# A pooling mixer's steps put in one written list, with its RMS norm and its spare accumulators rearranged

## The chip, the cores and the metric

The program runs on one core of a Trainium2 chip. The metric is the device time of one execution in microseconds (us); before the change its median over three executions is 1689.29 us. The engines meant below are TensorE (PE in the profile: matmuls and transposes, results into the PSUM accumulators), VectorE (DVE), ScalarE (ACT), GpSimd (POOL) and the DMA queues, of which SyncE's (SP) carries the weights. Each engine works through its own instructions in order and waits on semaphores for the others.

## The reference

One inference step of a two-layer decoder on 512 prompt tokens and 8 sample tokens (520 columns here), width 1024. Each layer is half a SwiGLU block, a token mixer, half a SwiGLU block. The mixer of layer 0 pools; that of layer 1 is sliding-window attention.

```python
x = x + 0.5 * _swiglu(_rmsnorm(x, norm_g[l, 0]), ...)
h = _rmsnorm(x, norm_g[l, 1])
# layer 0, _pool_mixer, for each of 4 groups of 256 channels with window w in (2, 4, 8, 16):
means.append((end[..., c0:c1] - start) / cnt)      # mean of the last w rows
diff = pooled - u                                  # (B, T, 4, 256)
mixed = einsum('btgc,gcd->btgd', diff, w_pool)     # a 256x256 product per group
out = mixed * scale
x = x + out
x = x + 0.5 * _swiglu(_rmsnorm(x, norm_g[l, 2]), ...)
```

## The kernel before

The residual lies transposed: eight tiles `x[m]` of 128 channels by 520 tokens. Matrix products keep fp32 accuracy by splitting each operand into a high and a low part (`xh`, `xl`; `wh`, `wl`): ACT copies the high part in the rounded type, DVE subtracts it from the source for the low part (`split`, lines 298 to 307), and PE does three products. Weights come in by SP, are split by ACT and DVE some pieces ahead of PE (`W.prefetch`, lines 226 and 227), and `W.stop` bounds how far ahead.

The stretch that the change touches starts in the last third of the first SwiGLU block (`ffn(0, ...)`, 344 to 372 us of the profile). For each `m` PE makes a down product, DVE multiplies it by the row of 1/rms (line 674, `u`) and adds it to `x[m]` (line 675), and `deferred` (line 711) splits `x[m]` for the mixer and adds its square to `acc` (lines 447 to 451). The last hidden tile of that block, `g`, is split into `hh` and `hl` at about 343 us and used by the first down products.

The mixer (lines 877 to 976) does for each of four groups: `zt`, thirty matmuls of 256 columns that multiply the tokens, in five parts of 128 (four of the prompt, a fifth for the last prompt rows and the samples), by the group's weights; `zt_evac`, five splits of these results scaled by 1/rms of each token (`zh` by ACT, `zl` by DVE); and `band`, which for each of two channel tiles does eleven matmuls with a band matrix (`th`, `tl`, `G`, `bt`) that does the pooling, two small ones for the samples, the addition to `x[m]` on DVE (lines 934 and 937), and the split of the new `x[m]` for the next block. `rstd_tok` sums `acc` over channels by five products with a column of ones (line 462) and takes 1/rms by a bit shift and three Newton steps on DVE. Two turned tiles (`hx`, lines 967 to 975) go out as the new pooling state.

What sets the order: a scheduler places every instruction on its engine by its own estimate of times, except those given to `later` (`keep_in_program_order`), which keep the written order among themselves. `seq` is `later` only while `ordered[0]` is true. The file defines `split` twice; the second definition, the one in force (lines 298 to 307 come from it), doesn't pass its two instructions through `seq`. In the mixer before, only the squares and a few steps are in written order. PSUM is eight banks, taken as four pairs (`duo`).

Of the kernel before, what the change touches and what calls it, by code (L numbers as in the profile page):

```python
# [18 lines left out]
P = 128  # L19
# [32 lines left out]
B_T = 520  # L52
B_W = 776

# [190 lines left out]
def yoco_step(ctx, tc, ins, outs):  # L245
# [33 lines left out]
    def seq(ins):  # L279

        return later(ins) if ordered[0] else ins
# [171 lines left out]
    pss_ = [None]  # L453
    nsb = [4]

    def rstd_tok(tiles=(0, P, 2 * P, 3 * P, 400)):
# [8 lines left out]
        seq(V.tensor_scalar(y.bitcast(I32), v.bitcast(I32), 1, None, op0=ALU.arith_shift_right))  # L465
        seq(V.tensor_scalar(y.bitcast(I32), y.bitcast(I32), -1.0, float(0x5F3759DF), op0=ALU.mult, op1=ALU.add))
        for it in range(3):
            seq(V.tensor_tensor(t_, y, y, op=ALU.mult))
            seq(V.scalar_tensor_tensor(t_, t_, -0.5, v, op0=ALU.mult, op1=ALU.mult))
            o = r_tok[:, :nt] if it == 2 else y  # L470
            seq(V.scalar_tensor_tensor(o, t_, 1.5, y, op0=ALU.add, op1=ALU.mult))

    def rstd_samples():
# [234 lines left out]
    def ff_pool():  # L708
        return tc.tile_pool(name="ff", bufs=2)

    def deferred(n, tmp, tag, tags, lst, w=TOK, hold=False):
# [166 lines left out]
    with tc.tile_pool(name="pm", bufs=2) as pm:  # L878
# [3 lines left out]
        tok0 = (0, 128, 256, 384, 400)  # L882
        r5 = pm.tile([P, 1], F32, name="r5", bufs=1)

        def zt(gi):

            pd = duo()
            banks = [pd[:, 0, :], pd[:, 1, :], ps()]
            wh, wl = prep["w", gi]
            views = []  # L890
            for tau in range(5):
                o = banks[tau // 2][:, (tau % 2) * 256 : (tau % 2) * 256 + 256]
                views.append(o)
                n = 0
                for kk in range(2):
                    xh, xl = mov1[2 * gi + kk]
                    s = slice(tok0[tau], tok0[tau] + P)
                    for a, b in ((xh, wh), (xh, wl), (xl, wh)):
                        T.matmul(o, a[:, s], b[:, kk, :], start=(n == 0), stop=(n == 5))  # L899
                        n += 1  # L900
            return views

        def zt_evac(views):
            zh = pm.tile([P, 5, 256], F32R, tag="zh", name="zh")
            zl = pm.tile([P, 5, 256], F32R, tag="zl", name="zl")
            for tau in range(5):
                split((zh[:, tau, :], zl[:, tau, :]), views[tau], r_tok[:, tau : tau + 1] if tau < 4 else r5)
            return zh, zl

        def band(gi, zz):  # L910

            zh, zl = zz
            Gt, (th, tl) = prep["G", gi], (prep["T", gi][:, 0, :], prep["T", gi][:, 1, :])
            G = lambda c: Gt[:, B_G + c : B_G + c + 256]
            for mi in range(2):
                m = 2 * gi + mi
                c = slice(mi * P, (mi + 1) * P)
                pd = duo()
                po, pso = pd[:, 0, :], pd[:, 1, :]
                pl = [(0, zh, th), (0, zl, th), (0, zh, tl), (1, zh, G(0)), (1, zl, G(0))]  # L920
                pr = [(1, zh, G(256)), (1, zl, G(256)), (2, zh, G(128)), (2, zl, G(128)), (3, zh, G(0)), (3, zl, G(0))]
                for half, lst in ((0, pl), (1, pr)):
                    for i, (tau, z, b) in enumerate(lst):
                        T.matmul(  # L924
                            po[:, half * 256 : half * 256 + 256],
                            z[:, tau, c],
                            b,
                            start=(i == 0),
                            stop=(i == len(lst) - 1),
                        )  # L930
                bs = Gt[:, B_S : B_S + NS]
                T.matmul(pso[:, :NS], zh[:, 4, c], bs, start=True, stop=False)
                T.matmul(pso[:, :NS], zl[:, 4, c], bs, start=False, stop=True)
                V.scalar_tensor_tensor(
                    x[m][:, SP:], pso[:, :NS], gcol(N_PS, m), x[m][:, SP:], op0=ALU.mult, op1=ALU.add
                )
                V.scalar_tensor_tensor(
                    x[m][:, :SP], po, gcol(N_PS, m), x[m][:, :SP], op0=ALU.mult, op1=ALU.add
                )
                z = pair(XX, [P, TOK])  # L940
                split(z, x[m], gcol(2, m))
                mov2.append(z)

        mov2 = []
        hx = pm.tile([P, KT, P], F32, name="hx", bufs=1)
        for k in range(KT):
            S.activation(hx[:, k, 0:120], x[k][:, 400:520], AF.Copy, scale=gcol(1, k))
# [19 lines left out]
        for a in range(2):  # L967
            pt = ps()
            for k in range(4):
                T.transpose(pt[:120, k * P : (k + 1) * P], hx[:, a * 4 + k, 0:120], ident)  # L970
            hrow = splp.tile([120, 512], F32, tag="S", name="hrow", bufs=4)
            S.activation(hrow, pt[:120, :], AF.Copy, scale=r_tok[:120, 4:5])
            cols = slice(a * 512, (a + 1) * 512)
            nc.gpsimd.dma_start(pool_prompt[0, 0, :, cols], hrow[97:112, :])
            nc.gpsimd.dma_start(pool_sample[0, :, 14, cols], hrow[112:120, :])

    movk = []
    with ff_pool() as tmp:
# [717 lines left out]
```

## Time and profile before

| | us |
|---|---|
| median of the runs (lowest, highest) | 1689.29 (1687.31, 1690.34) |
| the profiled execution | 1684.47 |
| span of its trace | 1682.70 |
| PE busy | 1652.9 (98%) |
| DVE busy | 1241.7 (74%) |
| ACT busy | 889.5 (53%) |
| mixer, from its first matmul to the next block's first | 33.49 |

The mixer's length is 405.67 less 372.18 in the timeline. A busy engine in the profile isn't one at its peak: matmuls overlap, so the time of one is read from start to start, and a wait from the bracket behind a row, which gives the engine's idle time before it and what ended it.

### The profile page before, as it was taken

The numbers are of one execution on the slowest core, as the hardware profiler recorded it, in microseconds if no ns is written. First come the engines' busy times: TensorE is split into PE (matmuls) and PEld (weight loads), VectorE is DVE, ScalarE is ACT, GpSimd is POOL, SyncE is SP. The second block draws the span as 40 slices with busy tenths as digits, with TensorE's granted clock in tenths as the row PEclk, the third lists the DMA queues.
The fourth block names the chain that finished last, engine by engine and source line by source line (L and its number), as shares of the span: only waits on it lengthen the run. The fifth ranks groups of instructions, "written<-read, shape, count | busy, mean of one in ns | idle before, by whom it ended". The sixth has DMA issues, their size and how long they took to land.

```text
span 1682.7 us, 34382 instructions
## 1 busy us (share of the span) xinstructions
PE 1652.9 (98%) x13740; PEld 1641.2 (98%) x13740; DVE 1241.7 (74%) x2371; ACT 889.5 (53%) x1766; POOL 151.9 (9%) x203
## 2 busy tenths in 40 slices
PE   9999999999999999999999999999989999999997
PEld 8999999999999999999999999999879999999997
DVE  6866866887975875878775875884886785785776
ACT  5743643666652552556552552653785663463455
POOL 0101101000101101100101101100100100110100
PEclk9999999999999999999999999999989999999999
DMA  8546846652645855634745845744212555675641
GB/s 215 137 124 142 188 128 136 172 166 76 147 134 128 178 146 128 166 114 119 167 132 125 190 131 129 164 144 106 66 26 76 131 124 141 138 169 145 143 126 51
DMA packets 314540, 225.97 MB, mean 134 GB/s; under 512 B 9726, under 2 KB 290022, under 8 KB 314340
## 3 DMA queue, kind: packets, MB, share of 16 engines
q1 hardware_dynamic: 287870, 178.12, 37.6%
q0 software_dynamic: 22752, 40.56, 14.9%
q10 hardware_dynamic: 3758, 5.09, 1.0%
q8 instruction: 108, 1.77, 0.4%
q14 instruction: 52, 0.43, 0.1%
HBM read 180.30 MB, written 5.04 MB: 110 GB/s over the span
## 4 chain that ended last, share of the span: by engine, by line
PE 94%; DVE 3%; ACT 2%; DMA 0%; issue 0%; ACTq 0%; DVEq 0%; SPq 0%; POOLq 0%
PE ps L524 45%; PE ps L498 42%; PE ps L1287 1%; ACT sm L1235 1%; PE ps L924 1%; PE ps L1257 1%; ACT xh L303 0%; PE ps L899 0%; PE ps L1203 0%; PE ps L1570 0%; PE ps L1577 0%; DVE wl L227 0%; PE ps L462 0%; PE ps L1381 0%; PE ps L783 0%
## 5 line engine op out<-in xcount | busy, mean ns | idle before, releaser
L226 ACT ACTIVATE wh<-raw 128x512 fp32r<-128x512 f32 (+1 forms) x730 | 442.9, 622 | 535.7 <-PE ps L498 319.1
L227 DVE TENSOR_TENSOR wl<-raw,wh 128x512 fp32r<-128x512 f32 (+1 forms) x730 | 484.1, 678 | 215.5 <-ACT wh L226 212.0
L524 PE MATMUL ps<-th,wh 128*128 128x260 f32 x1216 | 343.7, 283 | 0.0
L524 PE MATMUL ps<-tl,wh 128*128 128x260 f32 x1216 | 342.9, 282 | 0.0
L524 PE MATMUL ps<-th,wl 128*128 128x260 f32 x1216 | 341.4, 282 | 0.0
L498 PE MATMUL ps<-hh,wh 128*128 128x260 f32 x1340 | 271.4, 284 | 0.6 <-ACT vtok L1080 0.6
L498 PE MATMUL ps<-hl,wh 128*128 128x260 f32 x1340 | 271.4, 283 | 0.0
L498 PE MATMUL ps<-hh,wl 128*128 128x260 f32 x1340 | 269.1, 282 | 0.0
L524 PEld LDWEIGHTS ps<-tl,wh 128*128 128x128 f32 x1216 | 229.0, 188 | 0.0
L524 PEld LDWEIGHTS ps<-th,wh 128*128 128x128 f32 x1216 | 228.7, 188 | 0.0
L524 PEld LDWEIGHTS ps<-th,wl 128*128 128x128 f32 x1216 | 228.0, 188 | 0.0
L498 PEld LDWEIGHTS ps<-hl,wh 128*128 128x128 f32 x1340 | 207.7, 189 | 0.0
L498 PEld LDWEIGHTS ps<-hh,wh 128*128 128x128 f32 x1340 | 206.0, 189 | 1.2 <-ACT vtok L1080 0.9
L498 PEld LDWEIGHTS ps<-hh,wl 128*128 128x128 f32 x1340 | 206.6, 189 | 0.0
L524 PE MATMUL ps<-xh,wh 128*128 128x260 f32 x672 | 188.2, 283 | 0.0
L524 PE MATMUL ps<-xl,wh 128*128 128x260 f32 x672 | 188.0, 282 | 0.0
L524 PE MATMUL ps<-xh,wl 128*128 128x260 f32 x672 | 184.1, 281 | 0.0
L186 POOL DMA_DIRECT2D raw<-raw x76 | 65.5, 862 | 1297.5 <-DVE wl L227 484.8
L498 PE MATMUL ps<-xh,wh 128*128 128x260 f32 x736 | 149.1, 285 | 0.9 <-ACT wh L226 0.9
L498 PE MATMUL ps<-xl,wh 128*128 128x260 f32 x736 | 149.6, 284 | 0.2 <-DVE xl L802 0.2
L498 PE MATMUL ps<-xh,wl 128*128 128x260 f32 x736 | 147.9, 283 | 0.1
L674 DVE TENSOR_TENSOR u<-ps,R 128x520 f32<-128x520 f32 x93 | 64.9, 699 | 100.4 <-PE ps L498 100.4
(297 smaller groups left out, 2863.8 us busy)
## 6 DMA issues: line engine op xcount, KB each, us to landing
raw<-in_ffn_w_gate_dram SPq DMA_DIRECT2D x87, 512.0 KB, 3.9
raw<-in_ffn_w_up_dram SPq DMA_DIRECT2D x87, 512.0 KB, 5.4
raw<-in_ffn_w_down_dram SPq DMA_DIRECT2D x32, 1024.0 KB, 5.2
raw<-raw POOLq DMA_DIRECT2D x76, 256.0 KB, 3.3
S<-in_ffn_w_up_dram SPq DMA_DIRECT2D x76, 256.0 KB, 5.5
S<-raw POOLq DMA_DIRECT2D x76, 256.0 KB, 4.7
raw<-in_ffn_w_down_dram SPq DMA_DIRECT2D x16, 768.0 KB, 4.6
raw<-in_w_q_dram SPq DMA_DIRECT2D x8, 512.0 KB, 4.2
```

What stands on the lines that cost most here:

```text
L186: G.dma_start(blk(raw, 2, 1), blk(raw, 1, 1), accum_op=ALU.add)
L226: pin(nc.scalar.activation(dh, src, AF.Copy))
L227: pin(nc.vector.tensor_tensor(dl, src, dh.bitcast(F32), op=ALU.subtract))
L498: ins = T.matmul(banks[:, hf, :H], a[:, kk, :], hcols(b, hf), start=(first and i == 0), stop=(last and i == 2),)
L524: T.matmul(bank[:, :H], a[:, kk, :], b, start=(not more and kk == 0 and i == 0), stop=(kk == 3 and i == 2), skip_group_check=more,)
L674: pin(V.tensor_tensor(parts(u), bank[:, hfs[0] : hfs[-1] + 1, :H], parts(R[:, c]), op=ALU.mult))
L924: T.matmul(po[:, half * 256 : half * 256 + 256], z[:, tau, c], b, start=(i == 0), stop=(i == len(lst) - 1),)
L1235: S.activation(z, z, AF.Exp, scale=-1.0, bias=nm[:, i : i + 1], accum_out=self.den[:, i : i + 1])
L1257: T.transpose(both[:, bi, kt * 256 + e * P : kt * 256 + (e + 1) * P], self.sms[2 * bi + e][:, kt * P : (kt + 1) * P], ident,)
L1287: T.matmul(po[:, bi * 256 : (bi + 1) * 256], a, p_[:, kc_], start=(n == 0), stop=(n == 3 * len(kts) - 1),)
```

## The change

- A table `MPLAN` of 77 steps replaces the calls of the mixer. Each step is a letter and a number: Z and Y (a group's four parts and its fifth part), n (the norm), h (one copy into `hx`), e (one split of a result), B (a band), x (its addition to `x[m]`), s (the split of the new `x[m]`), q (its square), t (a turned tile), w (one piece of weights ahead), u (a load of the Silu table). While it runs, `seq` keeps the written order, so matmuls, additions, copies, squares and weight pieces are in it. The instructions of `split` (steps e and s) are not, for the reason above.
- The square of the last `x` tile is no longer added to `acc` by DVE. ACT writes it to a tile `held` (POOL clears its eight spare columns), and five more products with ones sum it.
- In this norm alone 1/rms comes from a square root on ACT, a reciprocal on DVE and one Newton step, in place of the shift and three steps. The Sqrt table is loaded by a step written behind the block's fourth down product; Silu's is loaded again by step u0.
- The four groups' fifth parts share one pair of banks, `fifth`, in place of a pair each.
- The five pieces of weights for the next block that were split without a fixed place come by steps w1 to w5.

```diff
+MPLAN = """
+h2 h0 Z0 h4 h5 Y0 n0 e0 h6 Z1 Y1 h3 e2 h1 Z2 e4 Y2 e9 e5 e1 e3 B0 h7 x0 e7 e6 s0 e8 B1 x1 e14
...
@@ rstd_tok
-        for t, lo in enumerate(tiles):
-            seq(T.matmul(pss[:, t : t + 1], acc[:, lo : lo + P], ones[:, 0:1], start=True, stop=True))
+        parts = [acc] if last is None else [acc, last]
+        for i, z in enumerate(parts):
+            for t, lo in enumerate(tiles):
+                o = pss[:, i * 8 + t : i * 8 + t + 1]
+                seq(T.matmul(o, z[:, lo : lo + P], ones[:, 0:1], start=True, stop=True))
...
+        if last is not None:
+            later(V.scalar_tensor_tensor(v, pss[:, 8 : 8 + nt], 1.0 / D, v, op0=ALU.mult, op1=ALU.add))
+            later(S.activation(y, v, AF.Sqrt))
+            later(V.reciprocal(y, y))
...
+        steps = 3 if last is None else 1
+        for it in range(steps):
@@ deferred
+            if hold and k == 3:
+                later(S.activation(warm, ones[:, 0:1], AF.Sqrt))
             if hold and k == KT - 1:
-                square(k, tmp, tag, later)
+                held.append(big.tile([P, TW], F32, tag="hh", name="held"))
+                nc.gpsimd.memset(held[0][:, TOK:], 0.0)
+                later(S.activation(held[0][:, :TOK], x[k], AF.Square))
@@ the mixer
+        def zt(gi, taus):
+            if gi not in zviews:
+                pd = duo()
+                zviews[gi] = [pd[:, tau // 2, tau % 2 * 256 : tau % 2 * 256 + 256] for tau in range(4)]
+            if 4 in taus:
+                if not fifth:
+                    fifth.append(duo())
+                zviews[gi].append(fifth[0][:, gi % 2, gi // 2 * 256 : gi // 2 * 256 + 256])
...
-        z0 = zt(0)
-        rstd_tok()
-        z1 = zt(1)
-        V.tensor_scalar(r5, r_tok[:, 4:5], sel[:, 32:33], sel[:, 33:34], op0=ALU.mult, op1=ALU.add)
-        e0 = zt_evac(z0)
-        z2 = zt(2)
-        e1 = zt_evac(z1)
-        band(0, e0)
-        z3 = zt(3)
-        e2 = zt_evac(z2)
-        W.stop = 10**9
-        W.prefetch()
-        W.pin = later
-        band(1, e1)
-        e3 = zt_evac(z3)
-        band(2, e2)
-        band(3, e3)
-        for m in range(KT):
-            square(m, pm, "sq", later)
+        def prefetch(i):
+            W.stop = W.ng - 1 + i
+            W.prefetch()
+        W.pin = later
+        ordered[0] = True
...
+            "q": lambda n: square(n, pm, "sq", later),
+            "t": hx_turn,
+            "w": prefetch,
+            "u": lambda n: later(S.activation(warm, ones[:, 0:1], AF.Silu)),
+        }
+        for step in MPLAN.split():
+            steps[step[0]](int(step[1:]))
+        ordered[0] = False
+        W.stop = 10**9
```

The order that the built programs have is shown below at three places. SP keeps its order throughout; PE, ACT and DVE keep theirs outside this stretch, the start of the block behind it and the attention stage.

**First place: ACT near the end of the first block.** `wh` is a piece of weights, `G` a band matrix, `pr` its raw tile, `hh` the high part of the last hidden tile. Before:

```order
L226 ACTIVATE wh<-raw_4201 128x384
L837 DMA pr<-in_bands_dram 128x512
L303 ACTIVATE hh<-g 128x520
L226 ACTIVATE wh<-raw_4201 128x384
L863 ACTIVATE G<-pr 128x512 x2
```

The same place now:

```order
L234 ACTIVATE wh<-raw_4201 128x384
L738 ACT_TABLE_LOAD
L738 ACTIVATE warm<-ones 128x1
L861 DMA pr<-in_bands_dram 128x512
L311 ACTIVATE hh<-g 128x520
L234 ACTIVATE wh<-raw_4201 128x384
L887 ACTIVATE G<-pr 128x512 x2
```

The Sqrt table's load stands three rows ahead of `hh`, though it is written behind the fourth down product.

**Second place: DVE in the mixer, from the first band's addition to the last low part of group 2.** `x_81` to `x_83` are the tiles m = 0 to 2; `zl` from `ps_5026` (before) and `ps_5019` (now) are group 2's, from `r_4918` and `r_4919` its fifth part. Before:

```order
L937 SCALAR_TENSOR_TENSOR x_82<-ps_5090,gT,x_82 128x512
L307 SCALAR_TENSOR_TENSOR xl<-x_81,gT,xh 128x520
L307 SCALAR_TENSOR_TENSOR zl<-ps_5026,r_tok,zh 128x256
L307 SCALAR_TENSOR_TENSOR zl<-ps_5027,r_4918,zh 128x256
L307 SCALAR_TENSOR_TENSOR xl<-x_82,gT,xh 128x520
L307 SCALAR_TENSOR_TENSOR zl<-ps_5026,r_tok,zh 128x256 x2
L934 SCALAR_TENSOR_TENSOR x_83<-ps_5180,gT,x_83 128x8
L937 SCALAR_TENSOR_TENSOR x_83<-ps_5180,gT,x_83 128x512
L307 SCALAR_TENSOR_TENSOR zl<-ps_5026,r_tok,zh 128x256
```

Now:

```order
L315 SCALAR_TENSOR_TENSOR xl<-x_82,gT,xh 128x520
L457 COPY acc<-sq 128x520
L315 SCALAR_TENSOR_TENSOR zl<-ps_5019,r_tok,zh 128x256
L235 TENSOR_TENSOR wl<-raw_4483,wh 128x512
L962 SCALAR_TENSOR_TENSOR x_83<-ps_5127,gT,x_83 128x8
L962 SCALAR_TENSOR_TENSOR x_83<-ps_5127,gT,x_83 128x512
L315 SCALAR_TENSOR_TENSOR zl<-ps_5019,r_tok,zh 128x256
L235 TENSOR_TENSOR wl<-raw_4483,wh 128x512 x2
L315 SCALAR_TENSOR_TENSOR xl<-x_83,gT,xh 128x520
L315 SCALAR_TENSOR_TENSOR zl<-ps_5019,r_tok,zh 128x256
```

Three pieces of weights and the first square's copy have come in between group 2's low parts.

**Third place: ACT in the attention stage, at about 1241 us.** `sm` is a softmax tile, multiplied by `den`; `oT` is the copy of a finished value product out of PSUM. Before:

```order
L303 ACTIVATE xh<-ps_16165 128x512
L1306 COPY oT<-ps_16196 64x256 x2
L1246 ACTIVATE sm<-sm,den 128x256 x2
L1363 ACTIVATE pr,smx<-ps_16206,smx 128x128
L1364 ACTIVATE smx<-sink_s,smx 128x1
```

Now:

```order
L311 ACTIVATE xh<-ps_16164 128x512
L1283 ACTIVATE sm<-sm,den 128x256 x2
L1343 COPY oT<-ps_16195 64x256 x2
L1400 ACTIVATE pr,smx<-ps_16205,smx 128x128
L1401 ACTIVATE smx<-sink_s,smx 128x1
```

The two multiplications have changed places with the two copies.

## Rows read from the trace of the kernel before

**Rows 1.** The page, part 1: busy us (share of span) and instructions.

```profile
PE 1652.9 (98%) x13740; PEld 1641.2 (98%) x13740; DVE 1241.7 (74%) x2371; ACT 889.5 (53%) x1766; POOL 151.9 (9%) x203
```

**Rows 2.** PE's waits, whole span: us in total, times, longest.

```profile
PE ps L462 <- DVE acc L451: 1.8, 1, 1.8
...
PE ps L1257 <- ACT oT L1306: 1.5, 1, 1.5
```

**Rows 3.** Timeline of PE in the mixer: start, us, instruction, [idle before <- releaser].

```profile
372.18 0.29 PE L899 MATMUL ps<-th,xh 128*128 128x256 f32 x1
...
375.62 0.28 PE L899 MATMUL ps<-th,xl 128*128 128x256 f32 x1
377.69 1.25 PE L462 MATMUL ps<-ones,acc 128*128 128x1 f32 x10 [1.79 <-DVE acc L451]
378.80 0.36 PE L899 MATMUL ps<-th,xh 128*128 128x256 f32 x1
...
383.38 0.39 PE L899 MATMUL ps<-th,xh 128*128 128x256 f32 x1 [0.81 <-DVE zl L307]
...
388.42 0.36 PE L924 MATMUL ps<-bt,zh 128*128 128x256 f32 x1
...
396.23 0.36 PE L924 MATMUL ps<-bt,zh 128*128 128x256 f32 x1 [1.07 <-DVE x L937]
...
404.08 0.65 PE L970 MATMUL ps<-ident,hx 128*120 128x128 f32 x4 [0.21 <-ACT hrow L972]
...
405.67 0.49 PE L498 MATMUL ps<-xh,wh 128*128 128x260 f32 x2
```

**Rows 4.** Timeline of DVE up to the norm's result.

```profile
372.20 1.30 DVE L227 TENSOR_TENSOR wl<-raw,wh 128x512 fp32r<-128x512 f32 x2
...
376.84 0.70 DVE L451 TENSOR_TENSOR acc<-acc,sq 128x520 f32<-128x520 f32 x1 [0.76 <-ACT sq L447]
...
381.29 0.17 DVE L471 SCALAR_TENSOR_TENSOR r_tok<-nt,ny 128x5 f32<-128x5 f32 x1
```

**Rows 5.** Timelines of ACT, DVE and PE at the last hidden tile.

```profile
343.31 0.64 ACT L303 ACTIVATE hh<-g 128x520 fp32r<-128x520 f32 x1
...
343.98 0.70 DVE L304 TENSOR_TENSOR hl<-g,hh 128x520 fp32r<-128x520 f32 x1
...
344.45 0.72 PE L498 MATMUL ps<-hh,wh 128*128 128x260 f32 x4
...
345.15 0.48 PE L498 MATMUL ps<-hl,wh 128*128 128x260 f32 x2
```

**Rows 6.** Timeline of ACT at a Sqrt table load in the last block.

```profile
1646.59 0.71 ACT L1500 ACTIVATE xg<-x,gT 128x520 f32<-128x520 f32 x1
1647.32 1.28 ACT L1506 ACT_TABLE_LOAD   x1
1648.62 0.20 ACT L1506 ACTIVATE warm<-ones 128x1 f32<-128x1 f32 x1
1648.72 0.25 ACT L1490 COPY ys<-ps 128x128 f32<-128x128 f32 x1
```

**Rows 7.** Timeline of DVE in the mixer: low parts, a band's addition, a new split.

```profile
384.66 1.90 DVE L307 SCALAR_TENSOR_TENSOR zl<-ps,r_tok,zh 128x256 fp32r<-128x256 f32 x4 [0.15 <-ACT zh L306]
388.60 0.23 DVE L934 SCALAR_TENSOR_TENSOR x<-ps,gT,x 128x8 f32<-128x8 f32 x1 [2.04 <-PE ps L933]
388.74 0.74 DVE L937 SCALAR_TENSOR_TENSOR x<-ps,gT,x 128x512 f32<-128x512 f32 x1
...
390.90 0.75 DVE L307 SCALAR_TENSOR_TENSOR xl<-x,gT,xh 128x520 fp32r<-128x520 f32 x1
```

**Rows 8.** Timeline of ACT in the attention stage.

```profile
1241.44 0.73 ACT L1306 COPY oT<-ps 64x256 f32<-64x256 f32 x2
1242.20 0.91 ACT L1246 ACTIVATE sm<-sm,den 128x256 f32<-128x256 f32 x2
```

**Rows 9.** Windows: us, busy of PE, PEld, DVE, ACT, POOL, granted clock, DMA.

```profile
1250.00:1260.00 10.00, 10.00 (x64) 9.85 (x64) 7.14 (x36) 7.40 (x29) 0.00 (x0) 0.66 0.38 88
```

More of the change, by code (lines that the diff above doesn't have):

```diff
@@ L454, in yoco_step, with rstd_tok @@
     nsb = [4]
-    def rstd_tok(tiles=(0, P, 2 * P, 3 * P, 400)):
+    def rstd_tok(tiles=(0, P, 2 * P, 3 * P, 400), last=None):
         pss_[0] = duo()
@@ L709, in ff_pool @@
         return tc.tile_pool(name="ff", bufs=2)
+    held = []
     def deferred(n, tmp, tag, tags, lst, w=TOK, hold=False):
@@ L898, in zt @@
                     for a, b in ((xh, wh), (xh, wl), (xl, wh)):
-                        T.matmul(o, a[:, s], b[:, kk, :], start=(n == 0), stop=(n == 5))
+                        seq(T.matmul(zviews[gi][tau], a[:, s], b[:, kk, :], start=(n == 0), stop=(n == 5)))
                         n += 1
[L901 to L908, printed above, removed]
@@ L910, in band, with zt_evac @@
-        def band(gi, zz):
-            zh, zl = zz
+        zs = {}
+        def zt_evac(gi, tau):
+            if gi not in zs:
+                zs[gi] = tuple(pm.tile([P, 5, 256], F32R, tag=n, name=n) for n in ("zh", "zl"))
+            r = r_tok[:, tau : tau + 1] if tau < 4 else r5
+            split(tuple(z[:, tau, :] for z in zs[gi]), zviews[gi][tau], r)
+        bands_ = {}
+        def band(m):
+            gi, mi = m // 2, m % 2
+            zh, zl = zs[gi]
             Gt, (th, tl) = prep["G", gi], (prep["T", gi][:, 0, :], prep["T", gi][:, 1, :])
@@ L914, in band @@
             G = lambda c: Gt[:, B_G + c : B_G + c + 256]
[L915 to L942, printed above, removed]
@@ new lines, in band @@
+            c = slice(mi * P, (mi + 1) * P)
+            pd = duo()
+            bands_[m] = po, pso = pd[:, 0, :], pd[:, 1, :]
+            pl = [(0, zh, th), (0, zl, th), (0, zh, tl), (1, zh, G(0)), (1, zl, G(0))]
+            pr = [(1, zh, G(256)), (1, zl, G(256)), (2, zh, G(128)), (2, zl, G(128)), (3, zh, G(0)), (3, zl, G(0))]
+            for half, lst in ((0, pl), (1, pr)):
+                for i, (tau, z, b) in enumerate(lst):
+                    o = po[:, half * 256 : half * 256 + 256]
+                    seq(T.matmul(o, z[:, tau, c], b, start=(i == 0), stop=(i == len(lst) - 1)))
@@ new lines, in band, with band_evac, band_split @@
+            bs = Gt[:, B_S : B_S + NS]
+            seq(T.matmul(pso[:, :NS], zh[:, 4, c], bs, start=True, stop=False))
+            seq(T.matmul(pso[:, :NS], zl[:, 4, c], bs, start=False, stop=True))
+        def band_evac(m):
+            po, pso = bands_.pop(m)
+            for c, p_ in ((slice(SP, TOK), pso[:, :NS]), (slice(0, SP), po)):
+                seq(V.scalar_tensor_tensor(x[m][:, c], p_, gcol(N_PS, m), x[m][:, c], op0=ALU.mult, op1=ALU.add))
+        def band_split(m):
+            z = pair(XX, [P, TOK])
+            split(z, x[m], gcol(2, m))
+            mov2.append(z)
@@ L959, in yoco_step, with hx_copy, norm @@
-        W.prefetch()
-        W.pin = later
-        band(1, e1)
-        e3 = zt_evac(z3)
-        band(2, e2)
-        band(3, e3)
-        for m in range(KT):
-            square(m, pm, "sq", later)
-        for a in range(2):
+        def hx_copy(k):
+            seq(S.activation(hx[:, k, 0:120], x[k][:, 400:520], AF.Copy, scale=gcol(1, k)))
+        def norm():
+            rstd_tok(last=held[0])
+            seq(V.tensor_scalar(r5, r_tok[:, 4:5], sel[:, 32:33], sel[:, 33:34], op0=ALU.mult, op1=ALU.add))
@@ L975, in yoco_step @@
             nc.gpsimd.dma_start(pool_sample[0, :, 14, cols], hrow[112:120, :])
+        def prefetch(i):
[3 more added lines that the diff above has]
+        ordered[0] = True
+        steps = {
+            "Z": lambda n: zt(n, range(4)),
+            "Y": lambda n: zt(n, (4,)),
+            "n": lambda n: norm(),
+            "h": hx_copy,
+            "e": lambda n: zt_evac(n // 5, n % 5),
+            "B": band,
+            "x": band_evac,
+            "s": band_split,
+            "q": lambda n: square(n, pm, "sq", later),
[7 more added lines that the diff above has]
+        W.stop = 10**9
     movk = []
```

27 lines of the change are left out of this document (12 added, 15 removed).

## The prediction

> **What bounds the kernel now.** I read the page first, then PE's waits, then the timelines of the stretch that is changed. PE is busy 98% of the span [rows 1], so a change pays where PE waits. In the mixer it does so four times [rows 3]: 1.79 us for the sum of squares, 0.81 for a low part, 1.07 for an addition to `x`, 0.21 for a turned tile. From its first matmul at 372.18 to the next block's first at 405.67 the mixer lasts 33.49 us. Nothing else in the change shortens PE's work, so the gain is bounded by the waits in this stretch. Read from start to start they are a little longer: the hole before the norm is 377.69 − 375.62 = 2.07, less 0.12 for the matmul itself, so 1.95; 0.16 more than the row's idle time. With as much added to the next two the four come to 3.88 + 0.48 = 4.4 us. That is 0.26% of the time, little over the 0.2% that a measurement of this kernel can tell from no change.
>
> **The change part by part.**
>
> *The norm's wait, and what comes in its place: −1.95 and +1.1.* Before, PE waited for DVE's last addition to `acc`, which itself waited for ACT's square [rows 2, 4]. Now the last square is not added but multiplied. It ends about where the addition began, 376.84, and the five pieces of weights that the scheduler had put between the last tiles, 0.65 us each [rows 4], move into the mixer, so DVE is earlier still unless it is held up elsewhere. PE gets to the norm at 375.74 at the earliest, spends some 1.1 us on the products with `acc`, and needs the square at 376.85. So this wait goes whole. The price is five more products: the ten records of the present five take 378.80 − 377.69 = 1.11 us [rows 3], so +1.1. The shorter chain behind it (about eight steps for thirteen; now 381.29 + 0.17 − 378.80 = 2.7 us after the products [rows 3, 4]) saves about 1 us, but PE has sixty matmuls of groups 1 and 2 to do meanwhile, some 7 us, so in itself it is worth nothing.
>
> *The other mixer waits: −2.45, and new ones: +2.6.* Sixty matmuls and not thirty now stand between the norm and the first band, so the waits of 0.81 and 1.07 go from where they are, and the turned tiles stand where their copies are long done. But DVE and ACT must do as much as before and more: four of the five pieces of weights, the first squares and a table load now come inside the bands. I priced the DVE rows of the second place by hand. From the norm to group 2's last low part DVE does fifteen low parts of 0.475 (1.90 for four), three band additions of about 0.9, three new splits of 0.75 [rows 7], three weight pieces of 0.65 [rows 4] and a copy of about 0.4: 7.1 + 2.7 + 2.25 + 1.95 + 0.4 = 14.4. The norm's chain of 1.6 and the first high part, 0.5, come ahead of it, and it idles about 1.7 before the first band's result, which stands behind the first ten low parts (it waited 2.04 there before [rows 7]): 18.2 in all. PE needs for its part 60 + 30 matmuls at 0.118 (thirty from 372.18 to 375.74) and four bands at 1.5 (388.42 is the second band's start, and thirteen matmuls follow): 10.6 + 6.0 = 16.6. So PE waits about 1.6 before the fifth band. Between the fifth and the seventh band PE has two bands and four turns, 3.7; DVE has five more low parts, an addition, a weight piece, a split and an addition to `acc`, 2.4 + 0.9 + 0.65 + 0.75 + 0.7 = 5.4, less what it has begun: another 1.2 to 1.7. These durations overlap by some 0.08 us from row to row (the first addition takes 0.23, but the next starts 0.14 after it [rows 7]); over the 28 and 10 rows that is 2.2 and 0.8 us back. The bounds are therefore 0.9 with all the overlap and 3.3 with none, and 4.4, the waits of before, if the two engines are held up as often as then. I take 2.6, nearer to the upper side, because the rows of before show these two engines in turn waiting for each other (0.15 and more a time), which the sum of durations leaves out.
>
> *The Sqrt table's load: +1.1.* It is placed three rows ahead of `hh`. At the nearest switch to this table [rows 6] ACT's next work starts 2.13 us after the start of the copy before it, 0.62 of which is the copy's own share: 1.5 us. `hh` would start at 343.31 + 1.5 = 344.8 and end at 345.46; PE wants it at 344.45 [rows 5]. The wait is 1.1 with the semaphore's delay. `hl` follows at once, 345.5 to 346.2, and PE, which takes 0.70 between its use of `hh` and of `hl`, finds it just done. DVE and ACT run behind PE for the rest of this block, so nothing hides that, and the whole remainder moves by 1.1. The bounds are 0, if ACT's waits for the band matrices come out earlier than before, and 1.5. The Trainium skill, on the page "ScalarE: Activation LUTs", section "What ACT_TABLE_LOAD costs", gives about 1.28 us for the load and about 1.38 more for a drain, 2.66 a switch. The load's 1.28 is the trace's; of a drain the rows show 0.1 us. By the skill's figure this term would be 2.5, and the sum 1.4 higher.
>
> *Attention: +0.8.* PE waits there 1.51 us for the copies `oT` [rows 2]. Now the two multiplications stand ahead of them, 0.91 us [rows 8], of which ACT overlaps about 0.1. Their inputs come no later than before. Bounds 0 and 0.9.
>
> *At no cost.* The fifth parts' common pair: a part is rewritten only a whole group of matmuls later, behind its evacuation. SP keeps its order; the weights of the fourth Strassen chunk are loaded some 25 us later because their buffer comes free when the last weight piece is split, but three plain tiles of PE's work, over 30 us, lie ahead of their use. POOL gets a clearing that nobody waits for.
>
> *Sum:* −4.4 + 1.1 + 2.6 + 1.1 + 0.8 = +1.2 us. On the profiled execution, 1684.47, that is 1685.7; the median of the runs lies 4.8 above it, so 1689.29 + 1.2 = **1690.5**.
>
> **The rivals.**
>
> *The list does what it is written for.* The four waits go, PE is never short of operands in the bands, and neither the table load nor the swap in the attention is felt because ACT reaches both early: −4.4 + 1.1 = −3.3, and 0.4 more if the turned tiles, which no longer alternate with band matmuls, run closer: 1685.6. For it: ACT is busy only 53% [rows 1]. Against it: the splits are not in the list, and DVE and ACT have more between the bands than before.
>
> *The norm's wait stays.* DVE is the late engine at the block's end and is now itself moved by the table load; if it loses the 1.5 us whole, the last tile is no earlier against PE and 1 to 1.9 us of the wait remain: 1692.0. Within 0.2%.
>
> *Slower: the clock.* In the attention stage PE's clock was granted at 0.66 over 1250 to 1260 [rows 9], that is, about 6.8 us at 1.2 GHz and not 2.4, behind a run of waits of which the 1.51 us one is the last large. Such a stretch costs half its length, 3.4 us. The waits in the mixer, up to 1.79, drew none. If the longer wait of 2.3 brings one stretch more of that length, the time is 1690.5 + 3.4 = 1693.9. It decides once some 4.4 us more are at the low level, since half of them is what the forecast leaves to 1692.7.
>
> *Slower: each switch holds ACT twice.* If ACT stands as long again as the load's own row, 1.28 us [rows 6], for each of the two loads, `hh` comes 2.4 us late, and Silu's load, which stands between the low parts of the last group, adds as much before the seventh band: 1690.5 + 2.6 = 1693.1. Rows 6 speak against it: what follows the load starts 1.30 after it. The rule of the Trainium skill cited above ("ScalarE: Activation LUTs") says that it is so.
>
> **How the numbers follow.** Forecast, within 0.2% (1685.9 to 1692.7): 0.61. The norm's wait stays, also within: 0.11. The list as written: 0.13, faster. The clock: 0.11, slower. The double hold: 0.04, slower. So faster 0.13, no change 0.72, slower 0.15. The unknown terms reach from 0.9 to 4.4 (bands), 0 to 1.5 (load), 0 to 0.9 (attention): 1686.9 with all low, 1692.8 with all high. To hold 8 in 10 the range takes in part of the cases on both sides, 1686.0 to 1694.0; it leaves out most of the first rival and the upper half of the clock's.
>
> **What would show it.** In the trace of the changed kernel: PE has no wait before the products with ones, which are twenty records over 2.2 us. PE waits about 1.1 us for `hh` at 344.5, behind a table load on ACT. PE waits one to one and a half us before the fifth and the seventh band, for `zl`. In the attention the wait for `oT` is 2.2 to 2.3 us. The forecast falls if the wait for `hh` is absent, if the bands run without a wait, or if the windows of the attention stage show more time at the low clock.

## The result

| | before | after |
|---|---|---|
| median of 22 runs, us (lowest, highest) | 1687.63 (1681.60, 1692.19) | 1692.22 (1685.88, 1694.99) |
| ratio, 95% interval | | 1.0024 (1.0012 to 1.0035) |
| the profiled execution, us | 1684.47 | 1690.16 |
| span of its trace, us | 1682.70 | 1688.3 |

The changed kernel is slower by 0.24%, 4.0 us (2.0 to 5.9). The forecast was 1.2 us slower, counted as no change within 0.2%; the measured time lies inside the range that was given and has the sign of the forecast, but it is three times as far and beyond the 0.2%, a case that the prediction gave 0.15. A second set of twelve runs of the changed kernel gave 1.0026 (1.0013 to 1.0040).

The executions of one kernel scatter over 9 to 11 us, and most of that goes with the granted clock: fitted over all runs of this study, an execution with 0.001 less in its mean granted clock is 1.2 to 1.3 us longer. The means agree, 0.9906 over 93 runs of the kernel before and 0.9905 over the 22 of the changed one, so the clock is not the difference. It does make two profiles hard to subtract: the traces hold stretches at the low level (granted clock 0.5), which lie elsewhere in each execution. Below, starts of the same matmul are compared only between such stretches.

### The profile page after: what moved, and what is told of

The parts are those of the page before. It is cut to its first block, busy times and chain, and to the rows that moved or that the text cites. A ratio compares the mean times of both kernels' runs of the same rounds, so it can differ in the third digit from the quotient of the medians.

```text
span 1688.3 us, 34402 instructions
## 1 busy us (share of the span) xinstructions
PE 1658.6 (98%) x13750; PEld 1646.5 (98%) x13750; DVE 1240.2 (73%) x2364; ACT 892.2 (53%) x1771; POOL 152.0 (9%) x204
## 4 chain that ended last, share of the span: by engine, by line
PE 92%; ACT 3%; DVE 3%; DMA 2%; issue 1%; ACTq 0%; POOL 0%; DVEq 0%; POOLq 0%; SPq 0%
PE ps L542 45%; PE ps L516 42%; PE ps L927 1%; ACT sm L1272 1%; PE ps L1324 1%; DMA S<-raw 1%; PE ps L954 1%; ACT wh L234 0%; ACT xh L311 0%; PE ps L1607 0%; PE ps L474 0%; PE ps L1240 0%; PE ps L1294 0%; DVE xl L312 0%; DMA S<-in_ffn_w_up_dram 0%
```

## The profile after

Part 1 of the page of the changed kernel, which answers to [rows 1]; PE is busy 5.7 us longer, in an execution that is 5.7 us longer:

```profile
PE 1658.6 (98%) x13750; PEld 1646.5 (98%) x13750; DVE 1240.2 (73%) x2364; ACT 892.2 (53%) x1771; POOL 152.0 (9%) x204
```

PE's waits in the changed kernel (us in total, times, longest), for [rows 2]. The wait for `acc` is gone; waits for `zl`, `wh` and `hh` are new. At the place of the attention stage where [rows 2] has 1.5 us for `oT` (line 1257, now 1294), PE waits 1.1 us for a low part of DVE's:

```profile
PE ps L954 <- DVE zl L315: 2.6, 2, 1.7
...
PE ps L542 <- ACT wh L234: 1.3, 2, 1.1
...
PE ps L1294 <- DVE xl L312: 1.1, 1, 1.1
...
PE ps L516 <- ACT hh L311: 0.7, 1, 0.7
```

Timelines at the last hidden tile, for [rows 5]. The load (1.28 us, as in [rows 6]) and the small activation behind it hold `hh` until 348.77, and PE stands idle 0.70:

```profile
347.36 1.28 ACT L738 ACT_TABLE_LOAD   x1
348.66 0.20 ACT L738 ACTIVATE warm<-ones 128x1 f32<-128x1 f32 x1
348.77 0.62 ACT L311 ACTIVATE hh<-g 128x520 fp32r<-128x520 f32 x1
...
349.44 0.74 PE L516 MATMUL ps<-hh,wh 128*128 128x260 f32 x4 [0.70 <-ACT hh L311]
```

From start to start the changed kernel falls 0.9 us further behind here: this row stands 4.99 behind its counterpart in [rows 5], the matmuls just before it 4.1.

Timeline of PE in the mixer, for [rows 3]:

```profile
377.42 0.28 PE L927 MATMUL ps<-th,xh 128*128 128x256 f32 x1
...
380.97 1.17 PE L474 MATMUL ps<-ones,acc 128*128 128x1 f32 x10
382.00 1.25 PE L474 MATMUL ps<-ones,held 128*128 128x1 f32 x10
383.11 0.37 PE L927 MATMUL ps<-th,xh 128*128 128x256 f32 x1
...
401.23 0.39 PE L954 MATMUL ps<-bt,zh 128*128 128x256 f32 x1 [0.90 <-DVE zl L315]
...
406.55 0.39 PE L954 MATMUL ps<-bt,zh 128*128 128x256 f32 x1 [1.74 <-DVE zl L315]
...
410.05 0.49 PE L516 MATMUL ps<-xh,wh 128*128 128x260 f32 x2
```

No bracket stands before the products; they take 383.11 − 380.97 = 2.14 us in place of 1.11. The four waits of before are replaced by two, before the fifth and the seventh band. The mixer lasts 410.05 − 377.42 = 32.63 us against 33.49: 0.86 shorter.

Forty microseconds later comes what the forecast did not have. Timelines of SP, POOL, ACT and PE, first before, then after:

```profile
372.93 0.37 SPq L318 DMA_DIRECT2D raw<-in_ffn_w_gate_dram  x1
...
376.95 16.54 SPq L989 DMA_DIRECT2D sink_s<-in_attn_sinks_dram  x8
416.84 0.39 SPq L318 DMA_DIRECT2D raw<-in_ffn_w_gate_dram  x1
...
435.22 1.83 POOL L185 DMA_DIRECT2D S<-raw  x2
```

```profile
404.34 0.37 SPq L326 DMA_DIRECT2D raw<-in_ffn_w_gate_dram  x1
...
408.64 15.56 SPq L1026 DMA_DIRECT2D sink_s<-in_attn_sinks_dram  x8
424.31 0.39 SPq L326 DMA_DIRECT2D raw<-in_ffn_w_gate_dram  x1
...
440.70 0.63 ACT L234 ACTIVATE wh<-S 128x512 fp32r<-128x512 f32 x1 [3.44 <-DMA S<-raw]
...
441.87 1.73 POOL L193 DMA_DIRECT2D S<-raw  x2 [2.14 <-PE ps L516]
...
450.87 0.39 PE L542 MATMUL ps<-xh,wh 128*128 128x260 f32 x1 [1.11 <-ACT wh L234]
```

SP's order is the same, but its first row here had to wait until the last weight piece was split, 404 and not 373. Twelve small copies (state, caches, sinks) stand behind that row, some 19 us of SP, and the next weights behind the copies. Before, the copies ran while SP had nothing else to do. Now they push the weights from 416.84 to 424.31. Part of that is the distance between the two profiles, so the places are better counted from the block's first matmul (405.67 and 410.05): the weights come 14.3 us behind it and not 11.2, POOL's sums `S` 31.8 and not 29.6. ACT stands 3.44 us for a piece of `S`, is then behind with its splits, and PE waits: 1.3 us from start to start.

## Experiments

Each ratio is to the kernel before on the same chip; 11 or 12 runs each, except the one noted. A time under the changed kernel "by the ratios" is taken from 1.0026, the second set on that chip, for the runs of the two edits, and from 1.0024 for the list with the old norm.

**The changed kernel again.**

> The changed kernel once more, beside the next three. Theory (places): its trace has the same three new waits of PE, 0.7 us for hh near 349 us, 2 and 1 us before two bands, 1.1 us for wh near 449.5 us, within 0.2 each, and the time is 1 to 4 us above the kernel before. Rival (clock): the places hardly matter, and the time goes with the mean granted clock: 0.990 to 0.992 here against 0.994 for the kernel before, 1.7 us for each 0.001.

1692.26 us, 1.0026 (1.0013 to 1.0040). The waits came back: 1.0 for `hh`, 2.7 for `zl`, 1.2 for `wh`. The mean granted clock of its runs is 0.9906. The clock rival falls, the places stand.

**The Sqrt load tied to the fourth square.**

```diff
-            if hold and k == 3:
-                later(S.activation(warm, ones[:, 0:1], AF.Sqrt))
...
+                sq = square(k, tmp, tag)
+            if hold and k == 3:
+                later(S.activation(warm, sq[:, 0:1], AF.Sqrt))
```

> The Sqrt table's load is tied to the fourth square, so that it can't be placed ahead of hh. Theory: PE's wait for hh near 349 us is gone (0.7 us idle, 0.85 in the starts), the load sits between squares where DVE is the later engine, and the time is 0.8 us under that of the changed kernel. Rival (late engine): the load now delays the squares, DVE's last addition comes 1 us later, PE waits for the products with ones again, 0.5 to 1.3 us, and nothing is gained.

1689.46 us, 1.0020 (1.0007 to 1.0033), 1.0 us under the changed kernel by the ratios. PE starts on `hh` without a wait, and none came before the products:

```profile
348.00 0.73 PE L517 MATMUL ps<-hh,wh 128*128 128x260 f32 x4
```

As the theory had it, for the trace; as a time 1.0 is less than the intervals can tell. The wait for `wh` near 449 us is absent in this profile too, though nothing was done to it. What explains it, as far as one trace can show, is a stretch at 1.2 GHz at the end of the mixer. Windows (us, busy of PE, PEld, DVE, ACT, POOL, granted clock, DMA) and PE's timeline there:

```profile
405.40:408.80 3.40, 3.40 (x19) 3.40 (x18) 3.40 (x8) 1.31 (x3) 1.08 (x2) 0.50 1.19 356
```

```profile
405.06 0.39 PE L955 MATMUL ps<-bt,zh 128*128 128x256 f32 x1 [1.77 <-DVE zl L315]
...
405.78 0.41 PE L955 MATMUL ps<-G,zl 128*128 128x256 f32 x1
406.00 0.41 PE L955 MATMUL ps<-G,zh 128*128 128x256 f32 x1
```

Two matmuls of 256 columns start 0.22 us apart here, against 0.12 at the high level, so the stretch cost PE some 1.5 us while SP, DVE and ACT went on. The late weights were then no longer late: one wait hid another. A wait that is absent from one profile is not proved cured.

**The copies ahead of the mixer.** The 12 DMAs of SP are written before the list, where SP waits for its buffer anyway.

```diff
+        later(nc.sync.dma_start(pool_sample[0, :, 0:14, :], state_pool[0, :, 1:15, :]))
...
         W.pin = later
         ordered[0] = True
...
-        later(nc.sync.dma_start(pool_sample[0, :, 0:14, :], state_pool[0, :, 1:15, :]))
```

> SP's copies of the state, the caches and the sinks (12 DMAs, some 15 us of SP) are written ahead of the mixer, where SP waits for a buffer, and not behind it. Theory (SP): the weights that followed the copies at 424 us come at about 409, the sum S on POOL by 427 and not 441, and PE's wait for wh at 449.5 us (1.1 us) goes: 1.1 us under the changed kernel. Rival (backlog): ACT and DVE are behind because four pieces were moved into the mixer; the sum comes early but PE waits 0.8 us or more for wh or hh in the same place.

1689.52 us, 1.0012 (1.0000 to 1.0024): 2.4 us under the changed kernel. The buffer comes free as late as there (402.85, in a profile that runs 1.5 us ahead of the changed kernel's here), but the weights behind it come at 417.88 and not 424.31, the sums at 436.80 and not 441.87; less the 1.5, that is 4.9 and 3.6 us earlier. PE has no wait between 444 and 452 us:

```profile
402.85 0.37 SPq L326 DMA_DIRECT2D raw<-in_ffn_w_gate_dram  x1
...
417.88 0.37 SPq L326 DMA_DIRECT2D raw<-in_ffn_w_gate_dram  x1
...
436.80 1.80 POOL L193 DMA_DIRECT2D S<-raw  x2
```

I had expected 409 for the weights and 427 for the sum; 436.80 was early enough. The wait for `hh` is still there, 1.13 us in this trace. The queue's copies were the cause, not a backlog of ACT.

**Both edits.**

> Both edits, the tied table load and the early copies. Theory (places): 2 us under the changed kernel, within 1.5 us of the kernel before on either side, and PE's starts behind 460 us stand where those of the kernel before stand, but for what the clock at the kernel's start makes. Rival (clock): the time stays with the changed kernel, 2 to 4 us above the kernel before, and its mean granted clock is 0.990 to 0.992.

1687.29 us, 1.0009 (0.9996 to 1.0023), 2.9 us under the changed kernel: the two edits add up within the intervals (1.0 and 2.4 alone). Neither wait is in its trace. Two thirds of the loss were these two waits, if the medians may be split so finely.

**The kernel before again, with a second profile.**

> The kernel before once more, with a profile of its own. Theory (places): outside the stretches at the low granted clock its PE stands within 0.3 us of the first profile of before all along, and the four waits of the mixer (1.8, 0.8, 1.1, 0.2) and that for oT in the attention return. Rival (one odd profile): the first profile was a lucky one, and this one is 1 to 3 us longer in stretches that the change does not touch, which would take as much from the difference between the two profiles.

1688.37 us, 0.9996 (0.9980 to 1.0011). Outside the low stretches and ahead of the attention stage its matmuls stand within 0.25 us of the first profile all along. So two profiles of one program can be laid on one another, and what is left over against the changed kernel needs a reason. In the attention they differ by 1 to 2 us. Its waits of PE:

```profile
PE ps L462 <- DVE acc L451: 2.3, 1, 2.3
...
PE ps L1257 <- ACT oT L1306: 0.6, 1, 0.6
```

The wait for `oT`, 1.5 in [rows 2], is 0.6 here in the same program. And behind the wait for `acc` there is a low stretch that the first profile did not have (window as above; it began at 381.9 and lasted 6.8 us):

```profile
381.00:389.00 8.00, 7.61 (x39) 7.64 (x40) 3.72 (x16) 3.44 (x12) 0.86 (x1) 0.57 0.77 279
```

**The list with the old norm.** The last square goes to `acc`, five products, shift and Newton steps; no table loads, no `held`.

```diff
-            rstd_tok(last=held[0])
+            rstd_tok()
...
-                held.append(big.tile([P, TW], F32, tag="hh", name="held"))
...
+                square(k, tmp, tag, later)
```

> The changed kernel with the norm of before: the last square is added to acc, five products, shift and three Newton steps, no table loads; the list stays. Theory (places): PE's wait for hh (0.85) and the five extra products (1.1) go, a wait for the last addition to acc comes back, 0.5 to 2 us, the longer chain costs nothing, the wait for wh near 449 us stays: 0 to 1.5 us under the changed kernel. Rival (norm pays): the wait comes back whole and the thirteen steps of DVE push the bands: 0.5 to 1.5 us above the changed kernel.

1690.30 us, 1.0012 (0.9997 to 1.0027), 2.0 us under the changed kernel. The wait before the products is back at 0.60 and a new one of 1.48 stands before the first band, whose splits now come behind the longer chain:

```profile
376.31 1.25 PE L474 MATMUL ps<-ones,acc 128*128 128x1 f32 x10 [0.60 <-DVE acc L459]
...
386.17 0.39 PE L950 MATMUL ps<-bt,zh 128*128 128x256 f32 x1 [1.48 <-DVE zl L315]
```

The wait for `wh` near 449 us, which the theory let stay, is 0.26 here. The mixer is as long as before. So the gain in the mixer is the new norm's, which the theory had wrong (the longer chain does cost), and yet the kernel without that norm is, if anything, faster. Part of that is the load. The rest showed when I laid this trace on the second one of before: they agree within 0.05 us from 43 us up to the mixer, and again from 454 us up to the attention, while the changed kernel's PE drifts away all along, in code that is the same. What does the new norm have that reaches so far?

**A wider buffer, and nothing else.** `held` is declared with 528 columns under the tag `hh`, whose other tiles have 520. One buffer size serves a tag, so all eight take 2112 bytes a partition, not 2080, and everything allocated behind them moves by up to 256 bytes. The same in the kernel before, by a tile of its last stage:

```diff
-        gB = big.tile([P, NH * P], F32, tag="hh", name="gB")
+        gB = big.tile([P, TW], F32, tag="hh", name="gB")[:, : NH * P]
```

> The kernel before with one tile of the tag hh, gB of the last stage, declared 528 columns wide and not 384: the same instructions in the same order, but each of the eight buffers of this tag takes 2112 bytes and not 2080, and hl, th, tl, xh, xl, raw, wh and wl lie up to 256 bytes further on. That is what the tile held (528 columns, tag hh) does in the changed kernel. Theory (addresses): PE's distance from start to start in the first block, 119.86 ns in both profiles of before and 120.10 in those of the changed kernel, becomes 120.10 here; outside the low-clock stretches the execution is 1.5 to 1.8 us longer than before. Rival (something else in the program, the list or the table loads): the distance stays 119.86 and the time that of before.

1690.36 us, 1.0019 (1.0005 to 1.0032): 3.2 us over the kernel before, with the same instructions. (Part of it can be the clock: the mean granted clock of these runs is 0.9900, that of the 35 runs of the kernel before beside them 0.9909, by the fit 1.1 us.) PE's timeline in the first block, the same two matmuls (2000 others from start to start) in before, after, and this run:

```profile
76.99 0.28 PE L524 MATMUL ps<-th,wl 128*128 128x260 f32 x1
...
316.36 0.28 PE L524 MATMUL ps<-tl,wh 128*128 128x260 f32 x1
```

```profile
80.53 0.28 PE L542 MATMUL ps<-th,wl 128*128 128x260 f32 x1
...
320.55 0.28 PE L542 MATMUL ps<-tl,wh 128*128 128x260 f32 x1
```

```profile
76.86 0.28 PE L524 MATMUL ps<-th,wl 128*128 128x260 f32 x1
...
316.88 0.28 PE L524 MATMUL ps<-tl,wh 128*128 128x260 f32 x1
```

239.37, 240.02 and 240.02 us: 0.64 more, at the high clock and without a wait in it. That is 119.69 and 120.01 ns from start to start over these 2000, other averages than the 119.86 and 120.10 of the expectation. Read so for all runs:

| matmuls of 260 columns, start to start, us | 2000 in the first block | 3000 in the last block |
|---|---|---|
| before, before again, old norm, old norm with early copies | 239.38 | 363.97 to 363.98 |
| after, after again, tied, early, both, pieces (below) | 240.02 | 364.34 |
| wider buffer | 240.02 | 364.83 |
| narrow `held`, rearranged list (both below) | 239.38 | 364.59 |

They fall on a few values that repeat to 0.01 us and go with the layout alone. For the whole kernel I laid each trace on the first one of before, matmul by matmul, in the stretches of the four SwiGLU blocks that hold no low clock and none of the waits that differ (43 to 372, 454 to 771, 850 to 1127 and 1277 to 1661 us of that trace). Traces of one layout agree within 0.03 us in each:

| us more than before | first | second | third | last | sum |
|---|---|---|---|---|---|
| before again, old norm, old norm with early copies | 0 | 0 | 0 | 0 | 0 |
| after, after again, tied, early, both, pieces (without the wait for `hh` and the low clock behind it) | 0.79 | 0.29 | −0.15 | 0.49 | 1.4 |
| wider buffer | 0.79 | 0.90 | −0.41 | 0.90 | 2.2 |
| narrow `held`, rearranged list | 0 | 0.67 | −0.10 | 0.65 | 1.2 |

That is 1.4 us for the changed kernel, and 2.2 for the wider buffer alone, where I had expected 1.5 to 1.8. In the third block the other layouts are faster than that of before. The Trainium skill, on the page "SBUF — State Buffer", section "Operand start alignment", asks only that an operand start at a multiple of its element size and says that this is about legality, not speed; both layouts keep it, and the speed differs.

**Both edits and `held` 520 columns wide.** The fifth product then has 120 rows and is added in the accumulator.

```diff
-                held.append(big.tile([P, TW], F32, tag="hh", name="held"))
+                held.append(big.tile([P, TOK], F32, tag="hh", name="held"))
...
+            seq(T.matmul(pss[: TOK - 400, 4:5], last[:, 400:], ones[:, 0:1], start=False, stop=True))
```

> Both edits (tied load, early copies) and held declared with 520 columns, the fifth product with ones adding its 120 rows to those of acc in the accumulator. Theory (addresses): PE's distance in the first block goes back to 119.86 ns; 1.6 us under the run of both edits, 0.5 to 1.5 us under the kernel before. Rival: distance and time stay with the run of both.

1685.18 us, 0.9986 (0.9974 to 0.9999), by the ratios 3.9 us under the run of both edits and 2.4 under the kernel before. The distance in the first block is that of before. In the later blocks it is not (second table): the layout costs 1.2 us in sum, hardly less than the 1.4 of the changed kernel. So the 1.6 us that the theory expected from the addresses are not in the trace, the cost has only moved to later blocks, and the 3.9 us are not shown to be the narrow buffer's. `held` still takes a turn among the eight buffers, so that later tiles lie in other ones; that this is the reason is argued, not tried alone. Caution with the gain: the mean granted clock of these runs is 0.9921, that of the 35 runs of the kernel before beside them 0.9909, which by the fit is 1.5 us; the run of both had 0.9905 beside 0.9908. Whether this kernel beats the one before is open; that it beats the changed one is not.

**The old norm and early copies.**

> The list with the norm of before and the early copies: no held, no table loads. Theory: addresses as before, no wait for hh and none for wh near 449 us; the mixer is as long as before (within 0.3), the list's gain being spent before the bands and the wait before the products kept: within 0.5 us of the kernel before. Rival (the list itself costs time that one profile doesn't show): 1.5 us or more above the kernel before, as the list with the old norm alone was (1.9 at equal mean clock).

1686.95 us, 0.9992 (0.9980 to 1.0005): the time of before, as the theory said, though the mixer is 0.6 longer there, by waits of 0.65 for `acc`, 1.84, 0.89 and 1.13 for `zl` and 0.37 for `x`. The list by itself, freed of what came with it, is worth nothing that shows.

**The weight pieces left to the scheduler.** `W.stop = 10**9` and `W.prefetch()` ahead of the list, steps w1 to w5 empty.

> The changed kernel with the five weight pieces left to the scheduler again, ahead of the mixer, and none in the list. Theory (late weights): SP loads the next weights near 375 us and not 404, PE's wait for wh near 449 us goes (1.3 to 1.8 us), the two waits before bands fall from 3.1 to under 2 us, and a wait of at most 1.3 comes before the products with ones: 1 to 3 us under the changed kernel. Rival (DVE late): the pieces hold up DVE's last additions, the wait for the last x tile or its square is 1.5 to 2 us and eats it: within 0.7 of the changed kernel.

1691.99 us, 1.0023 (1.0008 to 1.0038), no better than the changed kernel. The weights are early and the wait near 449 us is gone, none came before the products, and the wait before the fifth band is gone too. But the waits in the mixer did not shrink in sum (2.45 and 0.33 against 0.90 and 1.74), they gathered before the seventh band:

```profile
PE ps L954 <- DVE zl L315: 2.5, 1, 2.5
```

Four weight pieces of 0.65 us stand ahead of this band in the changed kernel's list and not here. DVE has 2.6 us less to do, so the amount of its work is not what ends this wait. The chain that does, followed back in the profile (start, us, what), passes through the load of Silu's table on ACT, step u0, which is line 1009 here:

```profile
400.70 1.28 ACT L1009
...
402.19 0.36 ACT zh L314
402.56 0.63 ACT xh L314
...
403.21 0.76 DVE xl L315
...
405.08 0.70 DVE acc L459
405.78 0.41 DVE zl L315
```

In the changed kernel the same load, at 401.21, stands in the chain that ends the wait of 1.74; in the two lists without table loads, those with the old norm, that wait is 1.11 and 1.13. Where the 1.3 us of the removed wait near 449 us went in the time I can't show; the intervals allow it.

**The splits in the list too.** `split` passes its two instructions through `seq`, on top of both edits; five runs, and the attention stage, which has a list of its own, is changed by it as well.

> Tied table load and early copies as in the run of both, and the splits' two instructions pass through seq too, so that ACT and DVE keep the list in them. Theory (scheduler's order): the two waits before bands (1.1 and 1.8 us) come of low parts that the scheduler put behind weight pieces and additions; in the list's order they fall to under 1.2 in sum, 1.5 us under the run of both. Rival (amount of work): DVE has too much to do between the norm and the last band in any order; the waits only move, and their sum is within 0.5 of 2.9.

1728.49 us, 1.0237 (1.0211 to 1.0263): 39 us slower, and both theories fall. In the mixer PE waits at seven places for ACT and DVE; the mixer is some 5 us longer, besides two low stretches of 10.2 us:

```profile
389.17 0.58 PE L955 MATMUL ps<-bt,zh 128*128 128x256 f32 x1 [2.90 <-DVE zl L315]
...
405.77 0.35 PE L955 MATMUL ps<-bt,zh 128*128 128x256 f32 x1 [1.94 <-DVE x L963]
...
410.19 0.38 PE L955 MATMUL ps<-bt,zh 128*128 128x256 f32 x1 [1.54 <-DVE zl L315]
```

So the list is only good with the splits left out of it, where the scheduler puts them between its steps. Which steps stand wrong for the splits was not sought. The attention lost more than the mixer: 30 us against 13 in this profile, set against that of both edits.

**Weight pieces and squares behind the last low parts.** Narrow `held`, both edits, and in the list:

```diff
-s1 q0 e12 e11 w1 B2 Z3 Y3 x2 e10 w2 w3 s2 B3 e17 x3 s3 e13 e18 w4 B4 e16 q1 e19 u0 q2 q3 x4 t0
-B5 s4 e15 B6 x5 x6 s5 B7 q4 q5 s6 x7 w5 s7 q6 t1 q7
+s1 e12 e11 B2 Z3 Y3 x2 e10 s2 w1 B3 e13 e17 x3 s3 e18 B4 e16 e19 e15 t0 B5 x4
+s4 w2 u0 q0 B6 x5 w3 q1 x6 s5 B7 q2 s6 x7 w4 s7 q3 q4 w5 q5 q6 t1 q7
```

> As the run with the narrow held, and in the list four weight pieces and the first squares stand behind the last low parts of groups 2 and 3, Silu's load behind the fifth band. Theory (DVE late before the bands): PE's waits of 1.1 and 2.0 us before the fifth and seventh band fall to under 0.8 in sum; the mixer is 2 us shorter, 2 to 3 us under the kernel before. Rival (work only moved): DVE is as late at the end, PE waits 1 to 2 us for the last xl in the next block's first tile, and the time is within 0.7 of the run with the narrow held.

1685.36 us, 0.9984 (0.9971 to 0.9998), that of the run with the narrow `held`. Its mean granted clock is 0.9928 beside 0.9909, so that by the fit most of the 2.7 us to the kernel before can be the clock. The waits before the bands fell to 0.21 and 0.88, and the difference came back where the next block starts:

```profile
399.48 0.38 PE L958 MATMUL ps<-bt,zh 128*128 128x256 f32 x1 [0.88 <-DVE zl L315]
...
404.95 0.47 PE L521 MATMUL ps<-xh,wh 128*128 128x260 f32 x2 [1.75 <-DVE x L966]
```

Together 0.21 + 0.88 + 1.75 = 2.84 us, and 2.7 in the run with the narrow `held`: the rival's case in the numbers, the waits only moved. But not because DVE is short of time. In the 8 us before this wait ends it stands idle 2.5 us for ACT, and the chain passes through Silu's load again:

```profile
401.52 1.28 ACT L1021 ACT_TABLE_LOAD   x1
...
403.58 0.43 DVE L457 COPY acc<-sq 128x520 f32<-128x520 f32 x1 [1.20 <-ACT sq L455]
```

So the load stands in the chain of the longest wait in each of the three placements (changed kernel, pieces ahead, this list). What the new norm would give with that load outside this stretch was not tried.

## Why the prediction was right or wrong

The steps that were costed held in size, but for the attention, which can't be told; two that were costed at nothing, or not seen, made the result.

- *The norm's wait, −1.95, and five products, +1.1:* right. No wait, 1.03 us more for the products. That the shorter chain behind them is worth nothing was wrong: with the longer one, in the run of the list with the old norm, PE waits 1.48 us before the first band, and here it does not.
- *The other mixer waits and the new ones, −2.45 and +2.6:* right in size: two waits, 0.90 and 1.74 idle, 1.15 and 1.99 in the starts, before the bands that were named. Forecast for the mixer −0.7, measured −0.86. For the first wait DVE's count was the right way to it: with the weight pieces out of the mixer it is gone. For the second the mechanism was half right. The count had DVE's rows alone; the table load on ACT was named there but had no price, and it stands in the chain that ends this wait, which did not shrink when DVE had the weight pieces no more. That 1.2 to 1.7 came so near is in part luck.
- *The Sqrt load, +1.1:* right; 0.9 from start to start, and gone when the load was tied. Of two holds by one switch the trace shows nothing: `hh` starts 1.41 us after the load.
- *Attention, +0.8:* can't be told. The term rested on a wait of 1.5 us that is 0.6 in another profile of the same program. One row of one execution was taken for a property of the kernel. The sign that was named, a wait of 2.2 to 2.3 for `oT`, did not come: at that place the two profiles of the changed kernel wait 1.09 and 2.14 for DVE's `xl`.
- *"At no cost", SP:* this step failed. The text saw that the weights would be loaded 25 us later and asked only whether the fourth chunk itself would be in time. It did not go on down the queue: behind that load stand 12 copies, which run some 19 us, and behind these the chunk after it. PE waits 1.3 us, and moving the copies gave back 2.4 by the ratios.
- *Not seen at all:* where `held` puts the other tiles. Its line was in the diff, with 528 columns where the tag has 520. It put the matmuls of the first block 0.3 ns further apart, well before the changed stretch begins, and cost some 1.4 us in all. The width is not all of it: with 520 columns the layout still cost 1.2.
- *The clock rival:* it did not happen, the mean clock is the same. Its argument was weak all the same: that the mixer's waits draw no low stretch was read from one profile, and the second has one of 6.8 us behind the same wait. Behind the new wait for `hh`, too, one begins in two of the four traces that have that wait (at 345.9 us in the second of the changed kernel, at 347.3 in that of the weight pieces).
- *The range:* it held, but its upper part was left open for the clock and the double hold, and neither came. That the late weights and the layout fell into the room left for them is luck.

With the measured values the sum is −0.9 + 0.9 + 1.3 + 1.4 = +2.7 us against 4.0 (2.0 to 5.9). What is left, 1.3, is inside the interval, and I give it no cause; the attention stage, where one program differs by 1 to 2 us from profile to profile, could hold it.

## To carry to other kernels

When a buffer comes free later, follow the whole queue behind the load that waits for it, down to the load after, and not only that load. When a tile joins a tag, it can move other tiles, by its width or by the turn that it takes: lay code that was not changed on the trace of before, matmul by matmul; here it was 0.1% of the time. When a wait only moves as the order is changed, follow the chain back from each place. The row that released PE was DVE's each time, and in all three placements the chain passed a table load on ACT that nobody had priced.

## What the hardware showed that I had not expected

The distance between two fp32 matmuls of 260 columns depends on where their operands lie in SBUF: 119.69 ns (239.38 us for 2000) in one layout and 120.01 in another that is 32 bytes wider for one tag, repeated to 0.01 us in 240 over six and eight traces. It goes either way: in the third block the second layout was 0.15 us faster over 276 us. Which address makes the difference was not sought.

A low stretch of the clock can hide a wait: PE lost some 1.5 us at 1.2 GHz in one run, the other engines and the queues went on, and the late weights were in time. The same program shows such stretches behind its waits in one execution and not in another, at about 382 us in the second profile of before and nowhere in the mixer of the first.
